# A one-hot scatter on three engines: half of the weighted rows go to ScalarE, the eviction changes its order, and 30 tiles are computed ahead

## The chip, the cores and the metric

The kernel runs on one core of a Trainium2 chip. Its time is the device time of one execution in microseconds; the kernel before has a median of 1787.21 us over three runs (1786.79 to 1787.54). The five engines are called TensorE (PE, with its weight loads PEld), VectorE (DVE), ScalarE (ACT), GpSimd (POOL) and SyncE (SP, which here only issues DMAs).

## The reference, cut to what matters

One layer of a diffusion backbone over 512 tokens of width 1024. A first half (pooling, retention, projections) ends with normalised tokens `hf`. Then comes PEER, a feed-forward net of 16384 single-neuron experts, of which each token uses 16 in each of 8 heads:

```
s  = einsum('thpd,hpkd->thpk', q, keys)          # 8 heads, 2 x 128 scores
s1, i1 = top_k(s[:, :, 0], 16); s2, i2 = top_k(s[:, :, 1], 16)
best, pos = top_k(all sums s1 + s2, 16);  eidx = i1 * 128 + i2 at pos
g   = softmax(best)
act = gelu(einsum('thkd,td->thk', u[eidx], hf))
out = einsum('thk,thkd->td', g * act, v[eidx])
```

The result is scaled by `g2`, added to `x`, and normalised once more.

## The kernel before, in words

Tokens are four blocks of 128. Block 0 is done as the reference says: its experts' rows are gathered by an indirect DMA and multiplied on VectorE. For the other three blocks (384 tokens, `NB * P`) the kernel is dense: it computes the activations of **all** 16384 experts, in 128 tiles of 128 experts, multiplies them by a matrix G that holds g for a chosen pair of token and expert and 0 elsewhere, and multiplies by all of v. A float32 product is three matmuls (`mm3`, L149 to L154) over parts `hi` and `lo` of each operand: `hi` is a cast on ScalarE (L164), `lo` a subtraction on VectorE or GpSimd (L169).

An *up tile* (`up_steps`) is 24 matmuls into PSUM and a Gelu on ScalarE that makes the tile `a` (L1138). It goes in two halves of 12 matmuls. 31 up tiles (`AHEAD`) are computed ahead of the main loop, wherever TensorE is expected to wait: `run_up(n)` issues n more halves, and the start of each tile also issues `prep`, the load and the split of the next one. A *down tile* is 18 matmuls into the six accumulators `Y`; `weigh(j)` multiplies `a` by its part of G and splits it into `ph` and `pl`, `run_v` loads and splits v tiles.

**The one-hot stage** (672 to 800 us) builds G. Each of 384 tokens has 128 chosen pairs (8 heads of 16), each with an index i1 and an index i2; the stage makes `o1`, one-hot rows of i1, and `o2`, one-hot rows of i2 times g, and a 128 x 128 matmul of the two gives that token's G. g is kept in two float16 parts, high and low, so o2 has two planes and each token two matmuls. It runs in 24 groups of 16 tokens (`NT`). `onehots` is four VectorE instructions of 2048 elements: `eq` (L1100), `o1` (L1101), and `eq` times the high and the low part (L1103, twice). `weights` is 32 matmuls and four evictions of 512 values on ScalarE (L1116), which write `st` so that the tokens of an expert stand side by side, and then a store from ScalarE's queue to the buffer `gd` (L1117). Each turn of the loop issues, in this order: the one-hots of the next group, one or two halves of up tiles, the matmuls and evictions of this group.

**Behind the stage** the kernel splits two more up tiles (`prep(k)`, `prep(k + 1)`), loads the first v tiles, reads G back, starts the top-k of block 0 (`tick`, whose VectorE work begins at L945), and runs the last ten halves between these steps. Then the **main loop** over j = 0 to 127 does a down tile each turn and the remaining up tiles spread over the turns to `JE`; the first step of block 0's `finish` (scale, add, square) is in its last turns. The down products of the last four tiles (`LAST`) are done block by block, and the blocks' `finish` follows.

All engines execute in the order in which the program issues: the kernel is written under a manual schedule. Dependencies are kept by semaphores, and buffers wait for their readers (`bufs`).

Of the kernel before, what the change touches and what calls it, by code (L numbers as in the profile page):

```python
# [36 lines left out]
GSCALE = 32768.0  # L37
NRAW = 3
NH = 2
AHEAD = 31  # L40
JE = 121
LATE = 118
LAST = 4
GATHER = 10
LAG = 2
CREDIT = 1.2
NT = 16
NI = 4
QU = 4
# [86 lines left out]
class Build:  # L136
# [627 lines left out]
    def heads(self, kp, s0, h0):  # L764
# [128 lines left out]
        next(last)  # L893
        nc.scalar.activation(self.gw, self.gw, AF.Exp)
        next(last)
        self.run_up(5)
        z = kp.tile([P, NB * PH], F32, name="z")
        self.softmax(self.gw, z, False)
        for _ in last:
# [132 lines left out]
    def finish(self, b, o, parts, x, g2, fg):  # L1032

        nc, gp = self.nc, self.dp
        ss = gp.tile([P, 4], F32, name="ss3", tag="ss3", bufs=3)
        S = [slice(0, 512), slice(512, D)]
        for s, src in zip(S, parts):
            nc.vector.tensor_tensor(o[:, s], src, g2[:, s], ALU.mult)
        for i, s in enumerate(S):
            nc.vector.tensor_tensor(o[:, s], o[:, s], x[:, s], ALU.add)  # L1040
            nc.scalar.activation(x[:, s], o[:, s], AF.Square, accum_out=ss[:, i:i + 1])
        yield
        nc.vector.tensor_tensor(ss[:, 2:3], ss[:, 0:1], ss[:, 1:2], ALU.add)
        self.rstd(ss[:, 3:4], ss[:, 2:3], 1.0 / D)
        yield
        for s in S:
            nc.vector.scalar_tensor_tensor(o[:, s], o[:, s], ss[:, 3:4], fg[:, s], ALU.mult, ALU.mult)
            nc.sync.dma_start(self.O["out"][b * P:(b + 1) * P, s], o[:, s])

    def routes(self, rp):  # L1050

        nc, dp = self.nc, self.rt
        N = NB * P
        ig = dp.tile([P, 4, N, NI], F16, name="ig", tag="ig", bufs=1)
        self.i12, self.gq = ig[:, 0:2], ig[:, 2:4]
        rep = [P, N, NI]
        ei = rp.tile([P, N], I32, name="ei", tag="qq", bufs=2)
        et = rp.tile([P, N], I32, name="et", tag="qq", bufs=2)
        ij = rp.tile([P, 2, N], F32, name="ij", tag="s", bufs=2)
        gT = rp.tile([P, 2, N], F32, name="gT", tag="s", bufs=2)[:, 0]  # L1060

        def turned(src):
            pt = self.ps()
            for b in range(NB):
                nc.tensor.transpose(pt[:, b * P:(b + 1) * P], src[:, b], self.ident)
            return pt[:, :N]

        nc.scalar.mul(gT, turned(self.gw), GSCALE)
        gT = gT.unsqueeze(2).to_broadcast(rep)
        nc.scalar.copy(self.gq[:, 0], gT)  # L1070
        nc.vector.tensor_copy(ei, self.ef.rearrange("p b k -> p (b k)"))
        nc.vector.tensor_scalar(et, ei, 7, None, ALU.logical_shift_right)
        nc.vector.tensor_scalar(ei, ei, 127, None, ALU.bitwise_and)
        nc.vector.tensor_copy(ij[:, 1], ei)
        nc.vector.tensor_copy(ij[:, 0], et)
        self.run_up(3)
        ij = ij.rearrange("p q (b k) -> p q b k", b=NB)
        i2 = turned(ij[:, 1])
        i1 = turned(ij[:, 0])
        nc.scalar.copy(self.i12[:, 0], i1.unsqueeze(2).to_broadcast(rep))  # L1080
        nc.vector.tensor_tensor(self.gq[:, 1], gT, self.gq[:, 0], ALU.subtract)
        nc.vector.tensor_copy(self.i12[:, 1], i2.unsqueeze(2).to_broadcast(rep))

    def onehots(self, t0, hp):

        nc = self.nc
        ts = slice(t0, t0 + NT)
        o1 = hp.tile([P, NT, P], F16, name="o1", tag="o1", bufs=NH)
        eq = hp.tile([P, NT, P], F16, name="eq", tag="eq", bufs=1)
        o2 = hp.tile([P, 2, NT, P], F16, name="o2", tag="o2", bufs=NH)  # L1090
        sh = [P, NT, P // NI, NI]

        def wide(o):
            return o.rearrange("p t (m i) -> p t m i", i=NI)

        def tokens(a):
            return a[:, ts].unsqueeze(2).to_broadcast(sh)

        row = self.ioh.rearrange("p (m i) -> p m i", i=NI).unsqueeze(1).to_broadcast(sh)
        nc.vector.tensor_tensor(wide(eq), row, tokens(self.i12[:, 1]), ALU.is_equal)  # L1100
        nc.vector.tensor_tensor(wide(o1), row, tokens(self.i12[:, 0]), ALU.is_equal)  # L1101
        for r in range(2):
            nc.vector.tensor_tensor(wide(o2[:, r]), wide(eq), tokens(self.gq[:, r]), ALU.mult)  # L1103
        return o1, o2

    def weights(self, t0, o, hp):

        nc = self.nc
        o1, o2 = o
        st = hp.tile([P, P, NT], F32, name="st", tag="st", bufs=2)  # L1110
        for t in range(0, NT, 4):
            ps = self.ps().rearrange("p (t m) -> p t m", m=P)
            for i in range(4):
                for r in range(2):
                    nc.tensor.matmul(ps[:, i], o1[:, t + i], o2[:, r, t + i], start=r == 0, stop=r == 1)  # L1115
            nc.scalar.mul(st[:, :, t:t + 4].rearrange("p m t -> p t m"), ps, 1.0 / GSCALE)  # L1116
        nc.scalar.dma_start(self.gd[:, t0 // NT], st)  # L1117


# [21 lines left out]
    def experts(self):  # L1141
# [5 lines left out]
        def place(p):  # L1147

            Gs[p] = (dp if p % 2 else self.g0).tile([P, N // NT, MG, NT], F32, name="G", tag="G", bufs=1)

        def read(p, b0=0, b1=N // NT):
            nc.sync.dma_start(Gs[p][:, b0:b1], self.gd[:, b0:b1, p * MG:(p + 1) * MG])

        def load_v(j):
            return self.load(I["uvd"][j, :, D:])
# [20 lines left out]
        def weigh(j, eng):  # L1176
            run_times(j + 1)
            a = acts.pop(j)
            if j < P - LAST:
                ph, pl = [dp.tile([P, N], F32R, name=x, tag=x, bufs=2) for x in ("ph", "pl")]  # L1180
            else:
                ph, pl = [self.ring.tile([P, N], F32R, name=x, tag="a", bufs=AHEAD + 1) for x in ("ph", "pl")]
            self.split(a, ph, pl, None, eng)
            return ph, pl

        def down(j, b, p, v):
            pb = [x[:, b * P:(b + 1) * P] for x in p]
            for h in range(2):
                s = slice(h * 512, (h + 1) * 512)
                self.mm3(Y[b][h], pb, [x[:, s] for x in v], j == 0, j == P - 1)  # L1190

# [8 lines left out]
        us, vs, ps = {}, {}, {}  # L1200
        nv = [0, 0]
        with tc.tile_pool(name="hot", bufs=1) as hp:
            oh = {}
            todo = list(range(0, N, NT))
            place(0)
            for i, t0 in enumerate(todo):
                for n in range(len(oh), min(i + NH, len(todo))):
                    oh[n] = self.onehots(todo[n], hp)
                self.run_up(2 if i % 3 == 0 else 1)
                self.weights(t0, oh[i], hp)  # L1210
                if i in (13, 20):
                    read(0, *{13: (0, 10), 20: (10, 18)}[i])
        self.rt_es.close()
        k = self.split_to
        self.prep(k, nc.vector)
        self.prep(k + 1, nc.vector)
        for n in range(2):
            vs[n] = load_v(n)
        nv[1] = 2
        read(0, 18, 22)  # L1220
        read(0, 22)
        self.dp = dp = self.pool("dense")
        place(1)
        tick()
        tick()
        self.run_up(3)
        self.prep(k + 2, nc.vector)
        tick()
        self.run_up(2)
        run_v(1, nc.gpsimd)  # L1230
        tick()
        acts.update(enumerate(self.acts))
        run_times(3)
# [15 lines left out]
            return min(P, AHEAD + (j + 1) * (P - AHEAD) // JE)  # L1249


        f0 = None

        for j in range(P):
            if j == GATHER:
                self.early.close()
                self.gp = es.enter_context(tc.tile_pool(name="gather", bufs=1, side="right"))
                self.acc = self.gp.tile([P, D], F32, name="acc", bufs=1)
            deep = j >= JE
            if j + 1 < P:  # L1260
                ps[j + 1] = weigh(j + 1, nc.vector)
            run_v(min(P, j + 4 if deep else j + 2), nc.vector)
            while nl < goal(j + 2):
                us[nl] = self.load_u(nl)
# [46 lines left out]
            if LATE < j <= LATE + 4:  # L1311
                b = j - LATE - 1
                nc.sync.dma_start(fin[2 + b], self.xd[b * P:(b + 1) * P])
            if j > LATE + 4 and done == S:
                if f0 is None:
                    f0 = self.finish(0, self.acc, [self.acc[:, 0:512], self.acc[:, 512:]], fin[2], fin[0], fin[1])
                    next(f0)
        for b in range(NB):
            for j in range(P - LAST, P):
                down(j, b, ps[j], vs[j])  # L1320
        assert not live and fetched == S
        last = [f0] + [self.finish(1 + b, self.wp.tile([P, D], F32, name="od", tag="raw", bufs=NRAW), Y[b],
                                   fin[3 + b], fin[0], fin[1]) for b in range(NB)]

        for b in (0, 0, 1, 1, 1, 2, 2, 2, 3, 3, 3):
            next(last[b], None)
        es.close()

# [12 lines left out]
```

## Time and profile before

| what | value |
|---|---|
| median of three runs | 1787.21 us |
| profiled execution, its own time | 1787.09 us |
| its span, first to last instruction | 1785.3 us |
| granted TensorE clock, mean | 0.987 |
| busy: PE, DVE, ACT, POOL | 1725.4, 1328.0, 777.2, 357.8 us |
| moved by DMA | 406.13 MB, 227 GB/s |

The busy times are of the span; the stages differ. [...] A row of a timeline has the start, the duration from first to last of the instructions merged in it, the engine, the line, the operation, output and inputs, the count, and in brackets the idle time of the engine before it with what ended that.

### The profile page before, as it was taken

Reading aid. Unit: us, or ns where it says so; the run is one execution under the profiler, and the core shown is the slowest. Engines: PE = TensorE matmul, PEld = TensorE weight load, DVE = VectorE, ACT = ScalarE, POOL = GpSimd, SP = SyncE. Lnnn points to the kernel's source line nnn. Section 1 sums busy time; section 2 is a strip of 40 time slices with the busy share of each in tenths; the row PEclk is TensorE's granted clock in tenths of the full one; section 3 lists DMA queues with packets and bytes.
Section 4 is the critical chain, followed back from the end, with each engine's and each line's share of the span. In section 5 each row is a group of like instructions: output and inputs, shape, how many; then the busy total and the mean of one; then the engine's idle time right before and its main releaser. Section 6 shows DMA issues by size and latency. Waiting matters only on the chain.

```text
span 1785.3 us, 26030 instructions
## 1 busy us (share of the span) xinstructions
PE 1725.4 (97%) x9882; PEld 1552.6 (87%) x9882; DVE 1328.0 (74%) x2408; ACT 777.2 (44%) x1320; POOL 357.8 (20%) x385
## 2 busy tenths in 40 slices
PE   6999999999989998997999999999999999999997
PEld 4899988888989997986889989999899998999995
DVE  7766365664468999988947788877888777888766
ACT  7443345222344347893344344443444434444343
POOL 0222230000026840004421111221111211212100
PEclk9999999999999999998999999999999999999999
DMA  8211134675332225774569989989899899989952
GB/s 321 101 48 48 60 124 128 214 250 182 111 138 77 95 81 192 273 286 143 162 239 360 334 310 321 328 308 343 309 319 331 317 333 319 315 324 314 345 188 106
DMA packets 134190, 406.13 MB, mean 227 GB/s; under 512 B 10896, under 2 KB 60336, under 8 KB 114480
## 3 DMA queue, kind: packets, MB, share of 16 engines
q1 hardware_dynamic: 111744, 243.50, 40.7%
q0 software_dynamic: 18432, 134.23, 20.1%
q10 hardware_dynamic: 3888, 26.74, 3.6%
q8 instruction: 77, 1.26, 0.3%
q14 instruction: 49, 0.40, 0.1%
HBM read 375.05 MB, written 29.38 MB: 227 GB/s over the span
## 4 chain that ended last, share of the span: by engine, by line
PE 81%; DVE 11%; issue 2%; ACT 2%; DMA 1%; POOL 0%; DVEq 0%; ACTq 0%; SPq 0%; POOLq 0%
PE ps L154 17%; PE ps L152 17%; PE ps L153 17%; PE Y L153 9%; PE Y L154 9%; PE Y L152 9%; DVE o L1103 3%; DVE lo L169 2%; DVE eq L1100 2%; PE ps L805 1%; DVE o L1101 1%; ACT hi L164 1%; DMA keys<-keys 0%; DMA raw<-uvd 0%; PE ps L693 0%
## 5 line engine op out<-in xcount | busy, mean ns | idle before, releaser
L169 DVE TENSOR_TENSOR lo<-raw,hi 128x1024 fp32r<-128x1024 f32 x297 | 365.3, 1231 | 79.9 <-ACT hi L164 77.0
L164 ACT CAST hi<-raw 128x1024 fp32r<-128x1024 f32 x332 | 343.4, 1050 | 179.0 <-DMA raw<-uvd 96.0
L152 PE MATMUL ps<-hfT,hi 128*128 128x384 f32 x1120 | 383.4, 342 | 11.8 <-ACT hi L164 10.4
L154 PE MATMUL ps<-hfT,lo 128*128 128x384 f32 x1120 | 381.7, 341 | 10.7 <-DVE lo L169 10.7
L153 PE MATMUL ps<-hfT,hi 128*128 128x384 f32 x1120 | 379.7, 339 | 1.6 <-DVE hfT L147 1.6
L152 PE MATMUL Y<-hi,ph 128*128 128x512 f32 x768 | 299.6, 390 | 3.5 <-ACT ph L146 3.0
L153 PE MATMUL Y<-lo,ph 128*128 128x512 f32 x768 | 301.5, 393 | 0.6 <-DVE lo L169 0.5
L154 PE MATMUL Y<-hi,pl 128*128 128x512 f32 x768 | 301.6, 393 | 0.1
L1011 POOL DMA_INDIRECT uv<-uv,eidx x128 | 154.3, 1206 | 638.5 <-DVE acc L1030 601.0
L152 PEld LDWEIGHTS ps<-hfT,hi 128*128 128x128 f32 x1120 | 213.8, 191 | 16.8 <-ACT hi L164 11.4
L154 PEld LDWEIGHTS ps<-hfT,lo 128*128 128x128 f32 x1120 | 213.7, 191 | 14.2 <-DVE lo L169 14.2
L153 PEld LDWEIGHTS ps<-hfT,hi 128*128 128x128 f32 x1120 | 214.1, 191 | 5.8 <-DVE hfT L147 2.0
L1138 ACT ACTIVATE a<-ps 128x384 f32<-128x384 f32 x128 | 62.9, 491 | 315.2 <-PE ps L154 311.9
L147 DVE TENSOR_TENSOR pl<-a,ph 128x384 fp32r<-128x384 f32 x128 | 70.9, 554 | 148.7 <-ACT ph L146 148.5
L152 PEld LDWEIGHTS Y<-hi,ph 128*128 128x128 f32 x768 | 144.5, 188 | 32.3 <-ACT ph L146 3.4
L154 PEld LDWEIGHTS Y<-hi,pl 128*128 128x128 f32 x768 | 144.5, 188 | 31.4 <-DVE pl L147 1.1
L153 PEld LDWEIGHTS Y<-lo,ph 128*128 128x128 f32 x768 | 144.4, 188 | 29.8 <-DVE lo L169 1.4
L1030 DVE SCALAR_TENSOR_TENSOR acc<-uv,act,acc 128x1024 f32<-128x1024 f32 x127 | 162.5, 1280 | 5.1
L1019 DVE SCALAR_TENSOR_TENSOR uv<-uv,hf 128x1024 f32<-128x1024 f32 x128 | 154.4, 1218 | 0.0
L169 POOL TENSOR_TENSOR lo<-raw,hi 128x1024 fp32r<-128x1024 f32 x35 | 85.5, 2451 | 236.7 <-ACT hi L164 226.6
L1116 ACT ACTIVATE st<-ps 128x512 f32<-128x512 f32 x96 | 91.4, 1115 | 9.7 <-PE ps L1115 8.3
L1021 ACT ACTIVATE act<-act 128x1 f32<-128x1 f32 x128 | 25.7, 201 | 145.7 <-DVE uv L1019 145.7
(287 smaller groups left out, 2870.8 us busy)
## 6 DMA issues: line engine op xcount, KB each, us to landing
raw<-uvd SPq DMA_DIRECT2D x252, 512.0 KB, 6.2
ada<-ada SPq DMA_DIRECT2D x48, 512.0 KB, 4.7
gd<-st ACTq DMA_DIRECT2D x24, 1024.0 KB, 4.8
raw<-w_in SPq DMA_DIRECT2D x44, 512.0 KB, 4.3
G<-gd SPq DMA_DIRECT2D x85, 256.0 KB, 7.0
raw<-wq SPq DMA_DIRECT2D x16, 512.0 KB, 3.9
raw<-ret_out SPq DMA_DIRECT2D x8, 512.0 KB, 4.8
raw<-w_out SPq DMA_DIRECT2D x8, 512.0 KB, 3.7
```

The source lines that it names most:

```text
L147: (eng_lo or nc.vector).tensor_tensor(lo, src, hi.bitcast(F32), ALU.subtract)
L152: mm(out, a[0], b[0], start=first, stop=False)
L153: mm(out, a[0], b[1], start=False, stop=False)
L154: mm(out, a[1], b[0], start=False, stop=last)
L164: self.nc.scalar.copy(hi, raw)
L169: eng.tensor_tensor(lo, raw, hi.bitcast(F32), ALU.subtract)
L1011: self.nc.gpsimd.indirect_dma_start(out=t, out_offset=None, in_=self.I["uv"], in_offset=bass.IndirectOffsetOnAxis(ap=self.eidx[:, s:s + 1] ...
L1019: nc.vector.scalar_tensor_tensor(t[:, :D], t[:, :D], 1.0, self.hf, ALU.mult, ALU.mult, accum_out=act[:, 0:1])
L1030: nc.vector.scalar_tensor_tensor(self.acc, t[:, D:], act[:, 1:2], self.acc, ALU.mult, ALU.add)
L1103: nc.vector.tensor_tensor(wide(o2[:, r]), wide(eq), tokens(self.gq[:, r]), ALU.mult)
L1116: nc.scalar.mul(st[:, :, t:t + 4].rearrange("p m t -> p t m"), ps, 1.0 / GSCALE)
L1138: nc.scalar.activation(a, ps[:, :N], AF.Gelu)
```

## The change

ScalarE makes the high weighted rows of the last eight of each 16 tokens: an activation `Copy` of one token's `eq` row with that token's column of `gT` as its scale (new function `weighted`, `NA = 8`). VectorE's product for the high plane covers only the first eight tokens. `eq` gets a second buffer, and `gT` moves from a short-lived pool into the ring of `a` tiles. The loop now issues the halves of up tiles first, then the next group's one-hots, then this group's matmuls and evictions, then the next group's weighted rows; two more tiles are split in its last two turns. The eviction reads PSUM in the order that `st` is written in, and no longer the other way round. `AHEAD` is 30 and not 31, with the halves dealt out anew (6 and 2 ahead of the loop for 5 and 3, 33 in it for 32, seven behind it for ten).

In the last turns `weigh` runs up to three tiles ahead, into tiles of the ring; block 0's `finish` leaves the main loop; the last four down tiles go by halves of `Y`; and `finish` does one half's product, sum and square before the other half's.

```
-AHEAD = 31
+AHEAD = 30
+NA = 8
-        self.run_up(5)                                   # heads, ahead of the softmax
+        self.run_up(6)
-        for s, src in zip(S, parts):                     # finish
+        for i, (s, src) in enumerate(zip(S, parts)):
             nc.vector.tensor_tensor(o[:, s], src, g2[:, s], ALU.mult)
-        for i, s in enumerate(S):
             nc.vector.tensor_tensor(o[:, s], o[:, s], x[:, s], ALU.add)
-        self.run_up(3)                                   # routes
+        self.run_up(2)
-        eq = hp.tile([P, NT, P], F16, name="eq", tag="eq", bufs=1)
+        eq = hp.tile([P, NT, P], F16, name="eq", tag="eq", bufs=NH)
-        for r in range(2):
-            nc.vector.tensor_tensor(wide(o2[:, r]), wide(eq), tokens(self.gq[:, r]), ALU.mult)
+        part = [P, NT - NA, P // NI, NI]
+        nc.vector.tensor_tensor(wide(o2[:, 0, :NT - NA]), wide(eq[:, :NT - NA]),
+                                self.gq[:, 0, t0:t0 + NT - NA].unsqueeze(2).to_broadcast(part), ALU.mult)
+        nc.vector.tensor_tensor(wide(o2[:, 1]), wide(eq), tokens(self.gq[:, 1]), ALU.mult)
+    def weighted(self, t0, o):
+        for t in range(NT - NA, NT):
+            self.nc.scalar.activation(o[1][:, 0, t], o[2][:, t], AF.Copy, scale=self.gT[:, t0 + t:t0 + t + 1])
-            nc.scalar.mul(st[:, :, t:t + 4].rearrange("p m t -> p t m"), ps, 1.0 / GSCALE)
+            nc.scalar.mul(st[:, :, t:t + 4], ps.rearrange("p t m -> p m t"), 1.0 / GSCALE)
             place(0)
+            oh = self.onehots(0, hp)
+            self.weighted(0, oh)
             for i, t0 in enumerate(todo):
-                for n in range(len(oh), min(i + NH, len(todo))):
-                    oh[n] = self.onehots(todo[n], hp)
-                self.run_up(2 if i % 3 == 0 else 1)
-                self.weights(t0, oh[i], hp)
+                self.run_up(1 if i % 3 or i == 3 else 2 if i else 4)
+                if i >= len(todo) - 2:
+                    self.prep(self.split_to, nc.vector)
+                now = oh
+                if i + 1 < len(todo):
+                    oh = self.onehots(todo[i + 1], hp)
+                self.weights(t0, now, hp)
+                if i + 1 < len(todo):
+                    self.weighted(todo[i + 1], oh)
-        k = self.split_to
-        self.prep(k, nc.vector)
-        self.prep(k + 1, nc.vector)
-        for n in range(2):
-            vs[n] = load_v(n)
-        nv[1] = 2
+        self.ask(AHEAD)
+        vs[0] = load_v(0)
         read(0, 18, 22)
         read(0, 22)
+        vs[1] = load_v(1)
+        nv[1] = 2
...
-            if j + 1 < P:
-                ps[j + 1] = weigh(j + 1, nc.vector)
+            for n in (j + 1, j + 2, j + 3) if j > P - LAST - 4 else (j + 1,):
+                if n < P and n not in ps and n >= j:
+                    ps[n] = weigh(n, nc.vector)
...
-            if j > LATE + 4 and done == S:
-                if f0 is None:
-                    f0 = self.finish(0, self.acc, ...)
-                    next(f0)
         for b in range(NB):
-            for j in range(P - LAST, P):
-                down(j, b, ps[j], vs[j])
+            for h in range(2):
+                for j in range(P - LAST, P):
+                    down(j, b, ps[j], vs[j], [h])
```

## Rows read from the trace of the kernel before

**Rows 1.** Windows of three stages: length; busy us (instructions) per engine; granted clock; DMA.
```profile
672.00:800.00 128.00, 114.97 (x1121) 107.64 (x1120) 126.55 (x111) 107.77 (x122) 0.00 (x0) 0.96 0.68 252
800.00:860.00 60.00, 49.42 (x246) 44.90 (x244) 48.19 (x193) 21.47 (x30) 25.63 (x79) 0.89 0.48 156
860.00:1740.00 880.00, 879.54 (x4386) 792.59 (x4385) 685.77 (x895) 363.72 (x682) 169.46 (x154) 1.00 0.87 308
```

**Rows 2.** Groups of instructions in 672 to 800: busy us, mean ns, idle before.
```profile
L1116 ACT ACTIVATE st<-ps 128x512 f32<-128x512 f32 x92 | 87.6, 1117 | 9.7 <-PE ps L1115 8.3 <-DMA gd<-st 1.4
...
L169 DVE TENSOR_TENSOR lo<-raw,hi 128x1024 fp32r<-128x1024 f32 x16 | 19.5, 1216 | 0.0
```

**Rows 3.** Timeline of ScalarE in the one-hot stage.
```profile
694.68 0.48 ACT L1138 ACTIVATE a<-ps 128x384 f32<-128x384 f32 x1
695.06 3.82 ACT L1116 ACTIVATE st<-ps 128x512 f32<-128x512 f32 x4
698.91 0.33 ACTq L1117 DMA_DIRECT2D gd<-st  x1
699.28 1.05 ACT L164 CAST hi<-raw 128x1024 fp32r<-128x1024 f32 x1 [0.40 <-ACT st L1116]
700.23 3.82 ACT L1116 ACTIVATE st<-ps 128x512 f32<-128x512 f32 x4
```

**Rows 4.** Timeline of VectorE, the first pair of weighted products.
```profile
672.79 2.35 DVE L1103 TENSOR_TENSOR o<-eq,ig 128x2048 f16<-128x2048 f16 x2
```

**Rows 5.** Groups of ScalarE over the span, shapes kept apart.
```profile
L1022 ACT ACTIVATE act<-act,gw 128x1 f32<-128x1 f32 x128 | 37.8, 295 | 4.2
L1021 ACT ACTIVATE act<-act 128x1 f32<-128x1 f32 x128 | 25.7, 201 | 145.7 <-DVE uv L1019 145.7
...
L696 ACT ACTIVATE ht<-ps,modc 128x128 f32<-128x128 f32 x12 | 5.0, 451 | 1.4 <-PE ps L693 1.3
...
L202 ACT COPY crow<-ps 128x512 f32<-128x512 f32 x4 | 2.1, 583 | 0.2 <-issue 0.2
```

**Rows 6.** Timeline of ScalarE, two runs of equal activations back to back.
```profile
10.89 1.54 ACT L202 COPY crow<-ps 128x512 f32<-128x512 f32 x3
...
490.08 0.79 ACT L696 ACTIVATE ht<-ps,modc 128x128 f32<-128x128 f32 x2
```

**Rows 7.** Timelines of ScalarE, VectorE and TensorE behind the one-hot stage.
```profile
801.46 3.73 ACT L1116 ACTIVATE st<-ps 128x512 f32<-128x512 f32 x4
...
806.72 2.36 DVE L169 TENSOR_TENSOR lo<-raw,hi 128x1024 fp32r<-128x1024 f32 x2 [7.89 <-ACT hi L164]
808.99 0.48 DVE L945 MAX8 sv<-s 128x8 f32<-128x128 f32 x2
...
829.39 1.22 DVE L169 TENSOR_TENSOR lo<-raw,hi 128x1024 fp32r<-128x1024 f32 x1 [0.49 <-ACT hi L164]
...
829.41 0.69 PE L152 MATMUL ps<-hfT,hi 128*128 128x384 f32 x1 [7.42 <-ACT hi L164]
...
837.49 0.50 PE L152 MATMUL Y<-hi,ph 128*128 128x512 f32 x1 [0.58 <-ACT a L1138]
...
837.87 0.56 DVE L147 TENSOR_TENSOR pl<-a,ph 128x384 fp32r<-128x384 f32 x1 [1.12 <-ACT ph L146]
838.83 1.23 DVE L169 TENSOR_TENSOR lo<-raw,hi 128x1024 fp32r<-128x1024 f32 x1 [0.39 <-ACT hi L164]
```

**Rows 8.** Timelines of TensorE and VectorE: the last up tile, and the tail.
```profile
1738.27 0.33 PE L152 MATMUL ps<-hfT,hi 128*128 128x384 f32 x1
...
1742.45 0.39 PE L152 MATMUL Y<-hi,ph 128*128 128x512 f32 x1
...
1759.27 0.50 PE L152 MATMUL Y<-hi,ph 128*128 128x512 f32 x1 [2.96 <-ACT ph L146]
...
1763.86 0.40 PE L154 MATMUL Y<-hi,pl 128*128 128x512 f32 x1
...
1777.58 1.28 DVE L1040 TENSOR_TENSOR od<-od,uv 128x512 f32<-128x512 f32 x2
```

More of the change, by code (lines that the diff above doesn't have):

```diff
@@ L1059, in routes @@
         ij = rp.tile([P, 2, N], F32, name="ij", tag="s", bufs=2)
-        gT = rp.tile([P, 2, N], F32, name="gT", tag="s", bufs=2)[:, 0]
+        self.gT = gT = self.ring.tile([P, N], F32, name="gT", tag="a", bufs=AHEAD + 1)
         def turned(src):
@@ L1101, in onehots @@
         nc.vector.tensor_tensor(wide(o1), row, tokens(self.i12[:, 0]), ALU.is_equal)
-        for r in range(2):
-            nc.vector.tensor_tensor(wide(o2[:, r]), wide(eq), tokens(self.gq[:, r]), ALU.mult)
-        return o1, o2
+        part = [P, NT - NA, P // NI, NI]
+        nc.vector.tensor_tensor(wide(o2[:, 0, :NT - NA]), wide(eq[:, :NT - NA]),
+                                self.gq[:, 0, t0:t0 + NT - NA].unsqueeze(2).to_broadcast(part), ALU.mult)
+        nc.vector.tensor_tensor(wide(o2[:, 1]), wide(eq), tokens(self.gq[:, 1]), ALU.mult)
+        return o1, o2, eq
+    def weighted(self, t0, o):
+        for t in range(NT - NA, NT):
+            self.nc.scalar.activation(o[1][:, 0, t], o[2][:, t], AF.Copy, scale=self.gT[:, t0 + t:t0 + t + 1])
     def weights(self, t0, o, hp):
         nc = self.nc
-        o1, o2 = o
+        o1, o2, _ = o
         st = hp.tile([P, P, NT], F32, name="st", tag="st", bufs=2)
@@ L1178, in weigh @@
             a = acts.pop(j)
-            if j < P - LAST:
+            if j < P - LAST - 2:
                 ph, pl = [dp.tile([P, N], F32R, name=x, tag=x, bufs=2) for x in ("ph", "pl")]
@@ L1184, in weigh, with down @@
             return ph, pl
-        def down(j, b, p, v):
+        def down(j, b, p, v, halves=(0, 1)):
             pb = [x[:, b * P:(b + 1) * P] for x in p]
-            for h in range(2):
+            for h in halves:
                 s = slice(h * 512, (h + 1) * 512)
@@ L1202, in experts @@
         with tc.tile_pool(name="hot", bufs=1) as hp:
-            oh = {}
             todo = list(range(0, N, NT))
             place(0)
+            oh = self.onehots(0, hp)
+            self.weighted(0, oh)
             for i, t0 in enumerate(todo):
-                for n in range(len(oh), min(i + NH, len(todo))):
-                    oh[n] = self.onehots(todo[n], hp)
-                self.run_up(2 if i % 3 == 0 else 1)
-                self.weights(t0, oh[i], hp)
+                self.run_up(1 if i % 3 or i == 3 else 2 if i else 4)
[7 more added lines that the diff above has]
+                    self.weighted(todo[i + 1], oh)
                 if i in (13, 20):
@@ L1226, in experts @@
         self.run_up(3)
-        self.prep(k + 2, nc.vector)
+        self.prep(self.split_to, nc.vector)
         tick()
@@ L1230, in experts @@
         run_v(1, nc.gpsimd)
+        self.prep(self.split_to, nc.vector)
         tick()
@@ L1249, in goal @@
             return min(P, AHEAD + (j + 1) * (P - AHEAD) // JE)
-        f0 = None
         for j in range(P):
@@ L1313, in experts @@
                 nc.sync.dma_start(fin[2 + b], self.xd[b * P:(b + 1) * P])
-            if j > LATE + 4 and done == S:
-                if f0 is None:
-                    f0 = self.finish(0, self.acc, [self.acc[:, 0:512], self.acc[:, 512:]], fin[2], fin[0], fin[1])
-                    next(f0)
         for b in range(NB):
-            for j in range(P - LAST, P):
-                down(j, b, ps[j], vs[j])
+            for h in range(2):
+                for j in range(P - LAST, P):
+                    down(j, b, ps[j], vs[j], [h])
         assert not live and fetched == S
-        last = [f0] + [self.finish(1 + b, self.wp.tile([P, D], F32, name="od", tag="raw", bufs=NRAW), Y[b],
+        last = [self.finish(0, self.acc, [self.acc[:, 0:512], self.acc[:, 512:]], fin[2], fin[0], fin[1])] + [self.finish(1 + b, self.wp.tile([P, D], F32, name="od", tag="raw", bufs=NRAW), Y[b],
                                    fin[3 + b], fin[0], fin[1]) for b in range(NB)]
-        for b in (0, 0, 1, 1, 1, 2, 2, 2, 3, 3, 3):
+        for b in (0, 0, 0, 1, 1, 1, 2, 2, 2, 3, 3, 3):
             next(last[b], None)
```

## The prediction, made before the change was built

> **What bounds the kernel now.** I read the windows by stage first, then the groups of the one-hot stage, then ScalarE and VectorE in order of time there, then the stretch behind it and the tail. From 860 to 1740 us TensorE is busy for 879.54 of 880 us at full clock [rows 1]: nothing is to be had there, and each matmul moved into it costs its own time. TensorE does the same matmuls before and after the change, so only its holes can pay: 13 us in 672 to 800, 10.6 us in 800 to 860, and the tail.
>
> In the one-hot stage (672 to 800) VectorE is busy for 126.55 of 128 us [rows 1], so it sets the pace, at 128/24 = 5.33 us for 16 tokens. ScalarE is second: 107.77 us busy, of which the 96 evictions L1116 take 1.117 us each [rows 2]. One turn of ScalarE shows a wait that does not count as busy: four evictions take 3.82 us, then the engine issues the store and nothing starts for 0.40 us, then a cast "hi" (0.95 us to the next start) or a Gelu (0.38 us) [rows 3]. That is 24 x (3.82 + 0.40) + 16 x 1.33 = 122.6 us of 128: an engine almost as full as VectorE. The change moves work from the one to the other, so ScalarE decides.
>
> **The change part by part.**
>
> *VectorE in the one-hot stage.* The second "eq" buffer lets VectorE write the next group while ScalarE still reads this one; without it the two would alternate. Two 2048-element products take 2.35 us, the second 1.13 us after the first [rows 4]. One of four such instructions becomes half as long: 0.57 us if it is all per element, 1.13 if nothing is saved; I take 0.60. A group then costs 3 x 1.13 + 0.60 = 3.99 us instead of 4.52, and with 18 "lo" at 1.13 (16 in the loop before, two more preps put into its last turns) the sum is 24 x 3.99 + 18 x 1.13 = 116 us.
>
> *The eviction.* Before, ScalarE reads PSUM in order and writes single words 64 bytes apart; now it reads words 512 bytes apart and writes four together. L202 evicts 512 contiguous values in 0.583 us, three of them in 1.54, so 0.48 us from start to start [rows 5, 6]. Ends: 0.90 a piece if the stride costs as much on the read side (the 3.82 us of rows 3), and 0.41 if not even L202's start cost is left. I take 0.48, the row that differs only in the stride: four evictions end after 3 x 0.48 + 0.58 = 2.02 us, 1.80 us a turn saved.
>
> *The weighted rows.* Eight activations of 128 values with a scale pointer per turn. Nearest is L696: 128 values with two pointers, 0.451 us, two in 0.79, so 0.34 apart [rows 5, 6]. One pointer less is worth L1022 minus L1021, 0.295 - 0.201 = 0.094 [rows 5], which leaves 0.25 us. Ends: 0.34, and 0.12 (128 values at the 0.92 ns by which 1024 values at 0.95 us exceed 512 at 0.48, no start cost). I take 0.25, 2.0 us a turn.
>
> [...]
>
> *ScalarE's sum.* The first turn now holds four halves of an up tile: tile 11 needs a "lo" that stands on VectorE behind the first one-hots. These start 670.5, and the end of the pair in rows 4 at 675.14 less 0.53 gives 674.6, the "lo" 675.8, the tile's 4.18 us of matmul [rows 8] 680. So evictions start at about 680.5, later than now, with two more halves done. From there 24 x 2.02 + 23 x 0.40 + 23 x 2.0 + 16 x 0.95 + 14 x 0.38 = 124.2 us, and the last eviction ends at 804.7 against 801.46 + 3.73 = 805.2 [rows 7]. ScalarE bounds the stage (124 us against VectorE's 116); the loop is hardly shorter. What was waited for behind it does change: VectorE stood 7.89 us for the casts behind the last evictions before it could start the top-k of block 0 at 808.99 [rows 7]. The last cast now stands ahead of the last evictions, ends near 802.7, and top-k starts near 804.0: **5.0 us earlier**. The wait added on VectorE, that "lo", holds back the last one-hots, which are queued behind it and for which ScalarE's last weighted rows wait; 1.2 us, inside ScalarE's 2.0 us of evictions.
>
> *Before the loop.* The half moved ahead of the softmax fills TensorE's hole there; VectorE's path to the first one-hots does not change. I count 0 (at most 2.1 us, one half, either way).
>
> *Behind the loop.* Seven halves are left there instead of ten, and the last tile is split ahead of the first down weights. Before, TensorE stood 7.42 us for that tile's cast at 829.41, ran it slowly, and the down products began at 837.49 [rows 7]. Now they can begin near 824.5 (829.39, where VectorE is through with the first weights, less 5), but the second tile's weights sit on VectorE behind a top-k step. There the waits of 0.49, 1.12 and 0.39 us and one "lo" of 1.14 go [rows 7], 3.1 us of VectorE time; TensorE, which now waits for that "lo" of 838.83 and not for its own late tile, gains 841.6 (837.49 and 18 products of 0.23) - (838.83 + 1.23 - 3.1) = 4.6. I take **4.0**, ends 2 (a slow start after its wait; the granted clock was 0.89 here [rows 1]) and 4.6. On SP's queue the second v load moves behind the two reads of G, which wait for the last store; that store leaves when it did, the tile is needed 30 us later, and I count nothing (if it is late, each us is one).
>
> *One tile fewer ahead.* It runs in the full loop: 1742.45 - 1738.27 = **4.2 us lost** [rows 8]. At nothing it would come only if the loop had holes, and rows 1 leave 0.5 us.
>
> *Tail.* TensorE waits 2.96 us at 1759.27 for a "ph" behind the squares of block 0's finish, and needs 4.59 us to 1763.86 for twelve matmuls worth 2.76 [rows 8]. Without finish(0) in the loop both go: 4.8 us. Late next: three weighings now stand ahead of the "lo" of the next down tiles, about 2 us on VectorE, and I charge 1.4 us for that and for the later loads that these release. The finish of the last block loses one add behind the last matmul, 0.6 us (half of 1.28) [rows 8]. Sum **4.0 us saved**, ends 0.6 and 5.4. The halves' order alone moves no matmul.
>
> *Sum*, against the profiled execution's own 1787.09 (span 1785.3, 1.8 around it; 0.12 under the median): -5.0 - 4.0 + 4.2 - 4.0 = -8.8, **1778**.
>
> **The rivals.**
>
> *A, slower: the strided read costs what the strided write did.* Place: L1116, 96 evictions on the engine that bounds the stage. Each 0.10 us on one adds 9.6 us. It eats the gain at 0.57 us a piece and makes the kernel slower than can be mistaken from 0.61; at the old 0.90 it adds 24 x 1.80 = 43 us: 1822. For it: no row shows a strided read of PSUM. Against: L1116 at 1.117 beside L202 at 0.583 differ in the write alone, so the read is not known to be to blame for anything. Between, at 0.61 to 0.75: 1791 to 1804.
>
> [...]
>
> *B, much faster: VectorE still bounds.* With evictions at 0.41 and rows at 0.20 or less ScalarE's sum falls under 110, VectorE's 116 us from 670.5 end near 788, and top-k starts 16 to 21 us earlier: 1762 to 1772. For it: two of my prices are the dear end of little-known ones. Against: TensorE itself is busy for 115 of the 128 us [rows 1] and gets one half more, and three engines so close to each other wait for one another.
>
> *C, no change: the two engines take turns.* In 16 of 24 turns a loop closes: cast (1.05), "lo" (1.22), "eq" (1.22), eight rows (2.1), next cast, about 6.0 us with the hand-overs, against ScalarE's own 5.75. That is 4 us; with rows at 0.28 instead of 0.25 another 5.5: up to 1788. For it: a half-full second engine was never needed so promptly before.
>
> **How the numbers follow.** Forecast (1772 to 1783.5) 0.44; B 0.13; C 0.18; A 0.17, and its halfway form 0.08. What a measurement can tell from no change is 0.2%, 3.6 us. Faster is 0.44 + 0.13 = 0.57, same 0.18, slower 0.25. The range runs from 1766 (B's lower half left out, 0.04) to 1803 (A proper left out, 0.17), 0.79; the forecast's own is 1772 to 1784.
>
> **What would show it.** Mean of L1116 near 0.58 and of the new rows near 0.35: the prices; L1116 above 0.70 is A. ScalarE fuller than VectorE between 680 and 800: the bound; the other way round is B. The first top-k instruction (L945) of block 0 near 804, the first product into Y near 825, the second tile's near 837. No wait of TensorE over 1.5 us behind 1755. I am wrong if the stage's ScalarE sum is off by over 10 us, or if the down products' start brings more or less than half of what I say.

## The result, and the profile after

The kernel after takes **1811.18 us** (median of four runs, 1808.41 to 1811.55), the one before 1787.38 (1786.79 to 1787.97): a ratio of 1.0128, 95% interval 1.0115 to 1.0140. The forecast was 1778.0 in a range from 1766 to 1803. The change makes the kernel slower by 23.8 us, and the forecast is wrong in sign.

The profiled execution of after has a span of 1809.0 us, 23.7 more than before. Five markers say where they were lost:

| marker | before | after | later by | forecast |
|---|---|---|---|---|
| last eviction of the one-hot stage ends | 805.19 | 826.10 | 20.9 | -0.5 |
| first top-k instruction of block 0 | 808.99 | 825.12 | 16.1 | -5.0 |
| second product of the third down tile | 850.21 | 865.53 | 15.3 | -9.0 |
| Gelu of the last up tile | 1742.65 | 1762.91 | 20.3 | -4.8 |
| end of the span | 1785.3 | 1809.0 | 23.7 | -8.8 |

So the stage gives 21 us of the error, the stretch behind it 3, the main loop 1, the tail 7. First the windows (length; busy us of PE, PEld, DVE, ACT, POOL; granted clock, the share of full speed that the profile shows for TensorE; DMA). The stage is taken up to its last eviction, before and then after, so that both windows hold all 24 groups but for VectorE's first instructions; the third line is the main loop of after.

```profile
672.00:805.19 133.19, 120.15 (x1159) 112.50 (x1157) 126.55 (x111) 112.55 (x127) 0.00 (x0) 0.96 0.69 254
672.00:826.10 154.10, 123.54 (x1145) 115.32 (x1146) 117.46 (x121) 130.06 (x321) 0.00 (x0) 0.93 0.63 224
860.00:1740.00 880.00, 877.99 (x4380) 791.19 (x4379) 691.50 (x941) 365.81 (x682) 174.30 (x180) 1.00 0.86 307
```

VectorE has fallen from 126.55 to 117.46 us, as it was meant to, and ScalarE has risen from 112.55 to 130.06. But **no engine's busy time fills the stage any more**: its window is 154.10 us, 21 us longer, and even with 0.40 us behind each of ScalarE's stores, 9 us in all, ScalarE is short of it. That is the look of a closed chain: each engine waits for another in turn. The groups of the stage in 672 to 800 give the prices and name the waits (busy us, mean ns of one, idle time before).

```profile
L1111 ACT ACTIVATE o<-eq,gT 128x128 f16<-128x128 f16 x159 | 48.6, 388 | 8.8 <-DVE eq L1100 5.9 <-ACT st L1123 1.2 <-DVE o L1103 1.2
L1123 ACT ACTIVATE st<-ps 128x512 f32<-128x512 f32 x78 | 41.0, 591 | 7.1 <-PE ps L1122 7.1
L170 DVE TENSOR_TENSOR lo<-raw,hi 128x1024 fp32r<-128x1024 f32 x14 | 17.2, 1226 | 30.8 <-ACT hi L165 30.7
L1103 DVE TENSOR_TENSOR o<-eq,ig 128x1024 f16<-128x1024 f16 x20 | 13.7, 687 | 0.0
```

The eviction (L1123) costs 0.591 us where it cost 1.117 [rows 2]; the half product (L1103) 0.687. The waits are in the third line: VectorE stands 30.7 us in front of "lo" for the cast "hi". ScalarE in order of time, two turns of the loop:

```profile
697.99 2.45 ACT L1111 ACTIVATE o<-eq,gT 128x128 f16<-128x128 f16 x8 [0.40 <-ACT st L1123]
700.34 1.03 ACT L165 CAST hi<-raw 128x1024 fp32r<-128x1024 f32 x1
701.27 2.03 ACT L1123 ACTIVATE st<-ps 128x512 f32<-128x512 f32 x4
...
703.80 2.44 ACT L1111 ACTIVATE o<-eq,gT 128x128 f16<-128x128 f16 x8 [0.50 <-DVE eq L1100]
706.15 0.47 ACT L1145 ACTIVATE a<-ps 128x384 f32<-128x384 f32 x1
707.40 0.60 ACT L1123 ACTIVATE st<-ps 128x512 f32<-128x512 f32 x1 [0.79 <-PE ps L1122]
...
710.96 2.45 ACT L1111 ACTIVATE o<-eq,gT 128x128 f16<-128x128 f16 x8 [0.40 <-DVE o L1105]
713.32 1.03 ACT L165 CAST hi<-raw 128x1024 fp32r<-128x1024 f32 x1
```

And VectorE in the same two turns:

```profile
701.40 1.23 DVE L170 TENSOR_TENSOR lo<-raw,hi 128x1024 fp32r<-128x1024 f32 x1 [3.89 <-ACT hi L165]
702.55 1.22 DVE L1100 TENSOR_TENSOR eq<-ioh,ig 128x2048 f16<-128x2048 f16 x1
...
705.42 1.22 DVE L1105 TENSOR_TENSOR o<-eq,ig 128x2048 f16<-128x2048 f16 x1
```

The reader follows one circle. The cast starts at 700.34, behind eight weighted rows; "lo" waits 3.89 us for it; all four one-hot instructions stand behind "lo" on VectorE (702.55 to 706.55); only then can TensorE make the products whose evictions run from 707.40 to 710.56; the next eight rows stand behind these on ScalarE, and the next cast (713.32) behind the rows. From cast to cast that is 12.98 us for two turns (11.99 near the end, from the cast at 810.92 to that at 822.91, where TensorE's granted clock is 1.00; from 700.34 to 713.32 it is 0.87), while ScalarE's own work in them is 2 x (2.35 + 2.06 + 0.40) + 0.94 + 0.37 = 10.9 and VectorE's 2 x 4.0 + 1.14 = 9.1. The chain of waits shows the same circle (start, us, what):

```profile
701.40 1.23 DVE lo L170
...
706.69 3.25 PE ps L1122 x31
711.27 2.14 ACT o L1111 x7
714.38 1.23 DVE lo L170
```

A second price rides on it. TensorE now waits in the stage, and behind some of its waits it is slow: in 706.5 to 710 the granted clock is 0.57, and the 31 matmuls from 706.69 take 3.25 us; from 817.27 as many take 1.89, in 817.2 to 819.3 the clock is 1.00, and the wait ahead of both is 0.90 us. What the clock costs over the whole stage was not measured by itself.

Behind the stage the rows that answer to [rows 7] are these: the last evictions, the start of top-k, the first down products, and three windows (two of after around its first down tile, and one of before around its own).

```profile
824.04 2.06 ACT L1123 ACTIVATE st<-ps 128x512 f32<-128x512 f32 x4
...
825.12 0.48 DVE L946 MAX8 sv<-s 128x8 f32<-128x128 f32 x2
...
847.96 0.79 PE L153 MATMUL Y<-hi,ph 128*128 128x512 f32 x1 [7.97 <-ACT a L1145]
854.87 0.40 PE L153 MATMUL Y<-hi,ph 128*128 128x512 f32 x1
856.17 0.50 PE L154 MATMUL Y<-lo,ph 128*128 128x512 f32 x1 [0.90 <-DVE lo L170]
865.53 0.50 PE L154 MATMUL Y<-lo,ph 128*128 128x512 f32 x1 [0.79 <-DVE lo L170]
```

```profile
847.90:851.00 3.10, 3.04 (x7) 2.47 (x8) 2.89 (x13) 2.29 (x4) 1.58 (x1) 0.50 0.00 0
851.00:854.90 3.90, 3.90 (x13) 2.97 (x12) 3.80 (x20) 0.05 (x1) 2.82 (x13) 0.65 0.00 0
```

```profile
837.40:841.70 4.30, 4.21 (x18) 3.49 (x19) 3.43 (x5) 2.36 (x5) 0.00 (x0) 1.00 0.10 25
```

From the first top-k instruction to the first down product after needs 22.84 us and before needed 28.50: 5.7 gained. But TensorE comes out of a wait of 7.97 us. Its first down tile takes 6.91 us (847.96 to 854.87) at a granted clock of 0.50 and 0.65; before it took 4.22 at 1.00. The next two tiles wait 0.90 and 0.79 for "lo". At the third tile 0.8 us is left of the gain.

### The profile page after: what moved, and what is told of

Its sections match the earlier page's. It is cut to its first block, busy times and chain, and to the rows that moved or that the text cites. A ratio compares the mean times of both kernels' runs of the same rounds, so it can differ in the third digit from the quotient of the medians.

```text
span 1809.0 us, 26197 instructions
## 1 busy us (share of the span) xinstructions
PE 1731.0 (96%) x9882; PEld 1556.2 (86%) x9882; DVE 1316.5 (73%) x2408; ACT 794.5 (44%) x1512; POOL 354.3 (20%) x385
## 4 chain that ended last, share of the span: by engine, by line
PE 51%; DVE 7%; ACT 4%; issue 1%; DMA 0%; POOL 0%; ACTq 0%; DVEq 0%; POOLq 0%
PE Y L154 9%; PE Y L155 9%; PE Y L153 9%; PE ps L155 8%; PE ps L153 8%; PE ps L154 8%; ACT o L1111 2%; DVE lo L170 2%; ACT hi L165 1%; DVE eq L1100 1%; PE ps L1122 1%; ACT st L1123 1%; DVE o L1105 1%; DVE o L1101 0%; DMA raw<-uvd 0%
## 5 line engine op out<-in xcount | busy, mean ns | idle before, releaser
L1012 POOL DMA_INDIRECT uv<-uv,eidx x128 | 150.3, 1174 | 646.7 <-DVE acc L1031 607.7
L153 PE MATMUL ps<-hx,hi 128*128 128x512 f32 x224 | 88.0, 393 | 1.1 <-ACT yTt L603 1.1
L155 PE MATMUL ps<-hx,lo 128*128 128x512 f32 x224 | 89.0, 397 | 0.0
```

What stands on the lines that cost most here:

```text
L153: mm(out, a[0], b[0], start=first, stop=False)
L155: mm(out, a[1], b[0], start=False, stop=last)
L1012: self.nc.gpsimd.indirect_dma_start(out=t, out_offset=None, in_=self.I["uv"], in_offset=bass.IndirectOffsetOnAxis(ap=self.eidx[:, s:s + 1] ...
```

## The experiments

Each is timed against the kernel before on the same chip; the medians of before were 1788.29, 1787.72 and 1787.53 us in the three batches. A ratio need not equal the quotient of the two medians exactly. "Rows" are the weighted rows on ScalarE.

**The order in the loop.** Only the place of the one-hots in the changed loop moves back ahead of the up tiles.

```
+                now = oh
+                if i + 1 < len(todo):
+                    oh = self.onehots(todo[i + 1], hp)
                 self.run_up(1 if i % 3 or i == 3 else 2 if i else 4)
...
-                now = oh
-                if i + 1 < len(todo):
-                    oh = self.onehots(todo[i + 1], hp)
                 self.weights(t0, now, hp)
```

> The changed kernel with one thing undone: the next group's one-hots are issued ahead of the halves of up tiles again, so no 'lo' stands before them on VectorE. Theory 1 (a closed chain sets the one-hot stage: cast 0.94, 'lo' 1.15, four one-hot instructions 4.0, products and evictions 3.2, store issue 0.4, eight weighted rows 2.35, next cast; 12.0 to 13.0 us per two turns, as the trace after shows): the chain opens, ScalarE's own sum (24 x 4.83 + 16 x 0.94 + 14 x 0.38 = 136 us) bounds, the last eviction ends near 815 instead of 826, the kernel takes about 1801. Theory 2 (ScalarE's prices alone set the stage): nothing to gain, 1808 to 1814.

Measured: 1801.24 us, ratio 1.0075 (1.0058 to 1.0091). The order alone is worth some 10 us of the 23.8. ScalarE in this kernel:

```profile
742.90 2.45 ACT L1111 ACTIVATE o<-eq,gT 128x128 f16<-128x128 f16 x8 [0.40 <-ACT st L1123]
745.25 1.03 ACT L165 CAST hi<-raw 128x1024 fp32r<-128x1024 f32 x1
746.19 2.03 ACT L1123 ACTIVATE st<-ps 128x512 f32<-128x512 f32 x4
```

No wait is left here but the 0.40 behind a store. The evictions run from 684.68 to 817.20 (an end near 815 was expected), 132.5 us; in the changed kernel they take 143.7 (682.4 to 826.1), so the circle cost 11.2 of them. The forecast's sum for this was 124.2; with the rows at the 2.35 us that the row at 742.90 shows up to the next start, and not 2.0, it is 124.2 + 23 x 0.35 = 132.2. Here ScalarE's own sum does bound the stage, as the forecast said, and it is longer than the whole stage was before (from the first eviction at 675.92 to 805.19, 129.3).

**The eviction alone**, in the kernel before.

```
-            nc.scalar.mul(st[:, :, t:t + 4].rearrange("p m t -> p t m"), ps, 1.0 / GSCALE)
+            nc.scalar.mul(st[:, :, t:t + 4], ps.rearrange("p t m -> p m t"), 1.0 / GSCALE)
```

> The kernel before with the new order of the eviction alone. Theory 1: an eviction costs 0.59 instead of 1.12 us, VectorE still bounds the stage, but the last evictions end about 3.5 us earlier, and with them the casts for which VectorE waits: the 7.89 us wait shrinks to about 4, 1783 to 1785. Rival (what ScalarE saves off the bound is worth nothing): 1786 to 1788.

Measured: 1784.12, ratio 0.9977 (0.9968 to 0.9987). The one part of the change that pays by itself: VectorE still sets the pace, but its wait ahead of top-k falls from 7.89 to 6.03 us (about 4 was expected); top-k starts at 806.62, 2.4 us earlier, the down products at 834.17, 3.3 earlier.

**No rows on ScalarE, with the changed order** (everything else as after).

```
-NA = 8
+NA = 0
-        part = [P, NT - NA, P // NI, NI]
-        nc.vector.tensor_tensor(wide(o2[:, 0, :NT - NA]), wide(eq[:, :NT - NA]), ...)
+        nc.vector.tensor_tensor(wide(o2[:, 0]), wide(eq), tokens(self.gq[:, 0]), ALU.mult)
```

> The changed kernel with all weighted rows back on VectorE (NA = 0), the loop's order and all else as changed. Theory 1: the chain loses 2.35 us of rows and gains 0.53 on VectorE, about 11 us per two turns; VectorE's sum (24 x 4.52 + 18 x 1.13 = 129 us) then nearly bounds; 1793 to 1799. Theory 2 (ScalarE's prices): ScalarE loses 56 us of work, the stage is VectorE's as it was before, and only the lost tile (4.2) and the tail (3.4) remain: 1787 to 1792.

Measured: 1791.42, ratio 1.0020 (1.0010 to 1.0029); top-k starts at 803.67. The first theory, that the order costs by itself, misses. Its window of the stage:

```profile
672.00:800.00 128.00, 112.33 (x1103) 105.62 (x1104) 123.27 (x109) 70.14 (x123) 0.00 (x0) 0.97 0.68 258
```

VectorE is nearly full again at 123.27 us. Without the eight rows the circle would be 11.99 - 2.35 + 0.53 = 10.2 us, the 0.53 being what the full product adds on VectorE (4.52 for 3.99); VectorE's own two turns take 10.2 with one "lo" and 11.3 with two. So the order costs little here. **The large loss takes both**: rows between the evictions and the next cast, and "lo" ahead of the one-hots. That the order costs nothing without the rows is not shown: the kernel with neither was not run, and the parts that were (the eviction at 1784.1, the tile at 1.4 and the tail at 2.2 us, both below) add up to 1787.7, 3.7 us less than this run.

**"lo" of the stage on GpSimd, in the changed kernel.** This opens the circle at another place than the first experiment: the order stays, but the one-hots no longer stand behind "lo".

```
+            self.lo_eng = nc.gpsimd
...
-                self.prep(j + 1, self.nc.vector)
+                self.prep(j + 1, self.lo_eng)
```

> The changed kernel with the 'lo' of the one-hot stage on GpSimd instead of VectorE; the loop's order is as changed. Theory 1 (the closed chain goes through 'lo' standing ahead of the one-hots on VectorE): opened in another way than by order, so as with the order undone: 1799 to 1803. If the order of ScalarE's and TensorE's instructions closes it, without VectorE's 'lo': 1808 to 1812. If GpSimd and VectorE hinder each other (a 'lo' above 2.5 us, one-hots above 1.25 us): 1803 to 1809.

Measured: 1799.58, ratio 1.0064 (1.0048 to 1.0081), as the first experiment within its interval. The stage's window, and VectorE's group "o1" in it:

```profile
672.00:800.00 128.00, 115.82 (x1011) 99.66 (x1012) 122.44 (x90) 111.95 (x283) 38.83 (x15) 0.97 0.64 232
```

```profile
L1102 DVE TENSOR_TENSOR o<-ioh,ig 128x2048 f16<-128x2048 f16 x23 | 58.5, 2543 | 1.4 <-PE ps L1123 1.4
```

Two ways to open the circle give the same time, and the same stretch of evictions (684.71 to 817.03, 132.3 us against 132.5), which is ScalarE's own sum of 132.2; in the window it is busy for 111.95 us, with 8.5 more behind stores. That "lo" ahead of the one-hots closes the circle, and that this costs some 10 us, is shown. The signs of the third theory are there too: a "lo" takes 2.59 us on average and "o1" 2.54 where it took 1.22, so some 30 of VectorE's 122.44 us (23 x 1.32) are the longer "o1" (more below). They did not make this kernel slower than the first experiment; ScalarE's sum is as long.

**Four rows, one-hots first, the tail of before.** The version that the first three point to: the cheap eviction, `NA = 4`, so that neither engine is overfull, and none of the tail's edits (those to `weigh`, `f0`, `down` and `finish`). 30 tiles ahead and the new dealing of the halves stay. The edit to the loop is that of the first experiment, of which only the added lines are shown.

```
-NA = 8
+NA = 4
...
+                now = oh
+                if i + 1 < len(todo):
+                    oh = self.onehots(todo[i + 1], hp)
                 self.run_up(1 if i % 3 or i == 3 else 2 if i else 4)
...
```

> The changed kernel with the one-hots issued ahead of the up tiles' halves, four weighted rows of 16 on ScalarE instead of eight, and the tail as before. Theory 1 (a row costs ScalarE 0.29 us and saves VectorE 0.07; balance at four, ScalarE 4.5 us and VectorE 5.1 us a turn): the stage is VectorE's, about 122 us, top-k starts 795 to 798 instead of 804 in the run with no rows; less 2 to 3 for the tail: 1780 to 1783. Rival (every row moved only adds hand-overs): 1787 to 1790.

Measured: **1781.72**, ratio 0.9967 (0.9956 to 0.9977): faster than both kernels by 6.0 and 29 us.

```profile
672.00:800.00 128.00, 114.89 (x1147) 108.47 (x1148) 121.10 (x113) 99.58 (x224) 0.00 (x0) 0.96 0.73 264
```

VectorE is nearly full again and ScalarE second. Top-k starts at 800.51, later than the 795 to 798 expected, the down products at 821.49. What the four rows add is not isolated: the eviction alone gave 4.2 of these 6.0 us, and the two intervals overlap (0.9968 to 0.9987 there).

**The same with "lo" on GpSimd**, to take the last of VectorE's load away (the last two diffs together).

> The kernel of e6 (one-hots first, four rows, tail as before) with the stage's 'lo' on GpSimd. By theory 1's sums VectorE has 24 x 4.27 = 102 us left in the stage, ScalarE about 108, TensorE 114: the stage shortens by some 6 us, 1774 to 1778. Rival (GpSimd hinders VectorE, or the 'lo' comes too late for TensorE): 1781 to 1790.

Measured: 1815.63, ratio 1.0154 (1.0137 to 1.0171), a miss of both theories. To see why, first GpSimd and VectorE in the changed kernel with "lo" on GpSimd:

```profile
729.38 2.49 POOL L170 TENSOR_TENSOR lo<-raw,hi 128x1024 fp32r<-128x1024 f32 x1 [8.27 <-ACT hi L165]
...
725.00 1.22 DVE L1102 TENSOR_TENSOR o<-ioh,ig 128x2048 f16<-128x2048 f16 x1
...
729.54 3.41 DVE L1102 TENSOR_TENSOR o<-ioh,ig 128x2048 f16<-128x2048 f16 x1
```

Then the version with four rows: GpSimd's group over the stage; a pair of its "lo" beside the first and the last of VectorE's instructions in the same time; and TensorE's wait for it (total, times, longest).

```profile
L170 POOL TENSOR_TENSOR lo<-raw,hi 128x1024 fp32r<-128x1024 f32 x13 | 62.8, 4845 | 88.4 <-ACT hi L165 67.3 <-PE ps L1124 21.1
```

```profile
751.45 10.03 POOL L170 TENSOR_TENSOR lo<-raw,hi 128x1024 fp32r<-128x1024 f32 x2 [10.98 <-ACT hi L165]
...
751.45 1.22 DVE L1102 TENSOR_TENSOR eq<-ioh,ig 128x2048 f16<-128x2048 f16 x1
...
755.73 1.22 DVE L1102 TENSOR_TENSOR eq<-ioh,ig 128x2048 f16<-128x2048 f16 x1
```

```profile
PE ps L155 <- POOL lo L170: 23.1, 5, 6.2
```

Where these instructions met, one or the other took longer. In the first fence VectorE's one-hot that starts 0.16 us behind GpSimd's "lo" takes 3.41 us and not 1.22: 2.33 until "lo" is over, and 1.08 behind it, near the 1.14 from one such instruction to the next. In the other kernel "lo" meets VectorE in an unbroken run of one-hots, from 751.45 to 756.95, none of which takes longer than alone; two "lo" need 10.03 us there, one at 738.10, while VectorE stands idle, 2.36, and the mean is 4.85 where it was 2.59. TensorE stands 23.1 us for them, and its granted clock is 0.88 in 672 to 800, where the version with "lo" on VectorE has 0.96. That the one engine waits for the other is the reading of these times; what makes it wait was not shown. The theory had priced "lo" as if GpSimd were free.

**One tile fewer ahead**, alone in the kernel before (`AHEAD = 30`).

> The kernel before with 30 tiles ahead instead of 31, nothing else. Theory 1 (a tile moved into the full main loop costs its 4.2 us, and the down products start hardly earlier, since the second tile's weights wait on VectorE): 1789 to 1791.5. Rival (behind the stage that tile runs at half clock and costs 8 us, of which the main loop asks 4.2 back): 1783 to 1786.

Measured: 1789.15, ratio 1.0010 (1.0001 to 1.0020): 1.4 us net. The tile's 4.2 us in the loop are partly paid back by the halves that no longer stand behind the stage: the down products start at 829.75 and not at 837.49, and at the second product of the third tile 3.3 us of that are left (846.96 against 850.21).

**The tail, in five versions.** All its edits in the kernel before; the same with block 0's `finish` left in the loop; the order by halves alone; weighing three ahead alone; and the version of four rows with the second of these tails. The edits are the change's own to `weigh`, `f0`, `down` and `finish`; "halves only" takes those to `down` and `finish`, "weighing three ahead only" those to `weigh`.

> The kernel before with the changes to the tail alone (weighing three ahead, finish of block 0 out of the main loop, halves of Y apart, finish by halves). Theory 1 (four finishes of 5.7 us follow one another on VectorE behind the last 'lo', and the first step of block 0's, which stood ahead of it, is now behind): 1789 to 1791. Rival (the tail is as good as forecast, and the 3.4 us that it lost in the changed kernel came from the state in which the stage left the loop): 1782 to 1787.

> The kernel before with the tail's changes but block 0's finish left in the main loop: weighing up to three ahead, halves of Y apart, finish by halves. Theory 1 (only the displaced finish cost time): 1785 to 1788.5. Rival (weighing ahead of the v tiles' split costs it): 1789 to 1791.5, as with all of the tail's changes.

> The kernel before with the last four down tiles by halves of Y and the finish by halves, and nothing else of the tail. Theory 1 (the order by halves asks for the last v tile after 9 products instead of 18, 2 us sooner, and it is not there): 1788.5 to 1790. Rival (weighing ahead is what costs; the order by halves only shortens the last finish by an add): 1786 to 1788.

> The kernel before with the weighing up to three tiles ahead (and its ring tiles), and nothing else of the tail. Theory 1 (the halves' order costs): 1786.5 to 1788.5. Rival (three weighings ahead of the v tiles' 'lo' put these and the loads they release about 1 to 2 us later): 1789 to 1791.

> The kernel of e6 (one-hots first, four rows) with the tail of e8 instead of the old one. Theory 1: the same distance from e6 as e8 has from the kernel before: 1778 to 1783. Rival (the tail as changed, but for the finish, costs 2 us): 1783 to 1786.

| kernel | us | ratio (95%) |
|---|---|---|
| before, all edits of the tail | 1790.46 | 1.0012 (1.0002 to 1.0021) |
| before, all but the displaced `finish` | 1790.74 | 1.0025 (1.0015 to 1.0035) |
| before, halves only | 1790.97 | 1.0017 (1.0007 to 1.0027) |
| before, weighing three ahead only | 1788.70 | 1.0008 (0.9999 to 1.0018) |
| four rows, tail edits but `finish` in the loop | 1785.09 | 0.9990 (0.9980 to 0.9999) |

No version of the tail gains anything, and the theory that the displaced `finish` is what costs fell twice (the second and the last row). The halves cost a little more than their theory's range, the weighing lies between its two. Why the halves cost is in VectorE's rows. First before, blocks 2 and 3; then halves only, block 1's second half and the same two blocks:

```profile
1770.95 1.28 DVE L1038 TENSOR_TENSOR od<-Y,uv 128x512 f32<-128x512 f32 x2
...
1776.38 1.28 DVE L1038 TENSOR_TENSOR od<-Y,uv 128x512 f32<-128x512 f32 x2
```

```profile
1769.93 0.69 DVE L1038 TENSOR_TENSOR od<-Y,uv 128x512 f32<-128x512 f32 x1 [1.72 <-PE Y L154]
...
1774.29 0.68 DVE L1038 TENSOR_TENSOR od<-Y,uv 128x512 f32<-128x512 f32 x1
1775.01 0.69 DVE L1039 TENSOR_TENSOR od<-od,uv 128x512 f32<-128x512 f32 x1
1775.62 0.68 DVE L1038 TENSOR_TENSOR od<-Y,uv 128x512 f32<-128x512 f32 x1
...
1779.97 0.68 DVE L1038 TENSOR_TENSOR od<-Y,uv 128x512 f32<-128x512 f32 x1
```

The blocks follow each other on VectorE without a wait for TensorE: 5.43 us from block to block before, 5.68 with halves, since a product and the add that needs it start 0.72 apart and two independent ones 0.60. Three blocks cost 0.75 us. The wait of 1.72 is new. A likely reason, not tested by itself: TensorE asks for the last of the four tiles after 9 products and not 18, and has 9 more still to do for block 1 when it comes, 9 x 0.23 = 2.1 us. In this execution the last Gelu, which stands ahead of the edit, is 0.87 later; the three make 3.3 of the 3.8 us by which the profiled span is longer.

## Why the prediction was wrong

The step that failed is ScalarE's sum, "24 x 2.02 + 23 x 0.40 + 23 x 2.0 + 16 x 0.95 + 14 x 0.38 = 124.2 us": it has no term for waits on another engine, and its rows were too cheap. From the first eviction to the last the stage took 143.7 us, of which 8.0 are the price of the rows and 11.5 the waits of a closed circle. Part by part:

*What bounds the kernel.* Right as far as it went: TensorE's loop has nothing to give, VectorE set the stage's pace, ScalarE decides.

*The eviction.* Right: 0.591 us against 0.58 taken. (Its lower end of 0.41, on which rival B rests, was a guess, worked out from no row, and no run shows it: four evictions at 2.03 us are 0.48 apart, (2.03 - 0.591)/3. And B's 16 to 21 us give 1762 to 1767 by the sum, not 1772. Neither bore on the result.) Rival A is out. The eviction that reads words 512 bytes apart took about what L202 takes for contiguous ones (0.591 us against 0.583).

*VectorE's half product.* Right: starts 0.60 apart (704.82 and 705.42).

*The weighted rows.* Mis-sized. "I take 0.25, 2.0 us a turn": measured 2.35 us a turn, (2.44 - 0.388)/7 = 0.293 us from start to start. The 0.25 was a spacing of 0.34 in the rows less a difference of two other rows, 0.094. What it left out costs 8 us (23 x 0.35), and by it alone ScalarE's sum (132 us) is beyond what the stage took before: with eight rows the change could not have gained there. The first experiment shows that sum.

*The loop: this step failed.* Rival C had the right kind of mechanism and the wrong circle: "cast, 'lo', 'eq', eight rows, next cast, about 6.0 us". It let the rows start behind "eq", but on ScalarE they stand behind this turn's evictions, those behind TensorE's products, and these behind all four one-hots, which stand behind "lo". The real circle spans two turns and takes 12.0 to 12.98 us. But for the products' time its parts stood in the rows of before or in the sums made from them: cast 0.95, "lo" 1.14, four one-hots 4.0, products and evictions 3 or so, store 0.40, rows 2.0. And "it holds back the last one-hots" was said of the last turns' "lo" alone; with the changed order it holds for every "lo" of the stage. Of the last eviction's 21.4 us (826.1 against 804.7), 1.9 are its start (682.4 against 680.5), 8.0 the rows' price, and the remaining 11.5 the waits of the circle. Undoing the order or moving "lo" away shortens the stretch from first to last eviction by 11.2 and 11.4, and the kernel by about 10.

*The start of top-k.* Its place was right: 1.0 us ahead of the last eviction's end, 0.7 forecast. It moved with the stage.

*Behind the loop.* 4.0 us forecast, 0.8 left. The hole and the late tile did go, 5.7 us, but the slow start that the text named for its lower end came whole (6.91 us for the first down tile against 4.22), and two waits for "lo" took most of the rest.

*One tile fewer.* 4.2 us forecast; from the third down tile to the last Gelu after takes 4.9 us longer, 4.2 of it the tile and the rest new holes (877.99 against 879.54 us busy in 880). By itself, with the halves dealt out as before, it costs 1.4, since what it frees behind the stage counts there.

*Tail.* 4.0 us saved forecast, 3.4 lost. "No wait of TensorE over 1.5 us" came true (the longest is 1.23, for a cast at 1780.85). It gained nothing, because the text read the tail from TensorE, and its end hangs on the last v tiles and then on VectorE. "The halves' order alone moves no matmul" failed too: with the finish by halves, that alone measured 3.4 us. The chain of waits in its last part, before and then after; the third fence is the issue of the same load in the kernel with the weighing alone:

```profile
1745.67 1.23 DVE lo L169
1746.91 5.85 DMA raw<-uvd
```

```profile
1768.01 1.23 DVE lo L170
1769.25 7.18 DMA raw<-uvd
```

```profile
1748.69 0.33 SPq L159 DMA_DIRECT2D raw<-uvd  x1
```

The load of a last v tile waits for a buffer that a "lo" sets free. Before, that "lo" ended 4.3 us behind the last Gelu; after, with weighings ahead of it, 6.3, and the load itself took 1.3 longer: together the 3.4. The weighing alone has the same 6.3 (its last Gelu is at 1742.36), so it is what puts the load 2 us later; why the load took longer is open. Which edit costs how much in time is not settled: alone the weighing costs 1.2 (its interval reaches to no change), the halves 3.4, and all together 2.2 in the kernel before.

## What to carry to other kernels

When work moves to a second engine, draw the circle before adding up the engines: follow one product through every queue it passes, to the next of its kind, counting what stands ahead of it in each queue and not only what it depends on. If no engine is full after a change and the stage is longer, look for a circle; moving one instruction in the issue order may then be worth more than its price. Compare such stages over the same work and not over the same microseconds. In the tail, read the chain of waits back from the last instruction before counting any engine's holes as time to be had.

## What had not been expected of the hardware

ScalarE read PSUM words 512 bytes apart at about the price of contiguous ones (0.591 us for 512 values against 0.583 of L202), while the eviction that read in order and wrote single words 64 bytes apart took nearly double (1.117). VectorE's one-hots and GpSimd's "lo", each with two inputs, got in each other's way: a one-hot of 1.22 us took 3.41 beside a "lo" of 2.49, and where VectorE had work without a break two "lo" took 10.03 us together, one beside an idle VectorE 2.36. In the tail with the halves alone a VectorE add that needs the product just ahead started 0.72 us after it (1774.29 to 1775.01), where two products that need nothing of each other started 0.60 apart before (512 values each), which is small but runs through a serial tail.
